# The decays' low-rank map as two float32 products, with the weights W and mu W, in a diffusion trunk with RWKV and neighbourhood attention

## The chip, the cores and the metric

The kernel runs on one core of a Trainium2 chip. The metric is the device time of one execution in microseconds (us); of several executions the median is given. TensorE multiplies matrices into PSUM; VectorE and ScalarE work element by element and may read PSUM; GpSimd works element by element on SBUF. The queues of SP and ScalarE issue the transfers. TensorE's clock has two levels here, 1.2 and 2.4 GHz.

## The reference, cut to what matters

The model has two layers, on 512 latent tokens and 128 context tokens of 1024 features. The first layer's mixer is RWKV-7. Its input h is the normalised x, scaled and shifted by the conditioning. Each of six users of h sees its own mixture of h and the difference delta between the neighbours' mean and h:

```python
def rms_norm(x, g):
    y = x32 * lax.rsqrt(jnp.mean(x32 * x32, axis=-1, keepdims=True) + NORM_EPS)
    return (y * g.astype(jnp.float32)).astype(x.dtype)
...
    h = modulate(rms_norm(xs, norm_g[l, 0]), sh1, sc1)
...
    delta = centred_token_shift(h) - h
    xs = h[None] + delta[None] * mu[:, None, None, :]
    rkv = jnp.einsum('ibtd,ide->ibte', xs[:3], w_rkv)
    r, k, v = rkv[0], rkv[1], rkv[2]
    xw, xa, xg = xs[3], xs[4], xs[5]
    g = jax.nn.sigmoid(xg @ g1) @ g2
    for d in range(2):
        z = w0[d] + jnp.tanh(xw @ w1[d]) @ w2[d]
        decay = jnp.exp(-jnp.exp(-jax.nn.softplus(-z) - 0.5))
        a = jax.nn.sigmoid(a0[d] + (xa @ a1[d]) @ a2[d])
```

The change concerns `xw @ w1[d]`, the first factor of the decays' low-rank map. The two directions' 64 columns each stand side by side, so W is 1024 by 128 there. The scan over the tokens, the output projection, the MLP and the second layer (attention and MLP) follow.

## The kernel before, in words

Activations lie with the features on the 128 partitions: a feature block k (KT = 8 of them) of all T = 640 tokens is one 128x640 piece, and a product of weights with them runs as two halves of HALF = 320 tokens, each into a PSUM bank.

Products with large weights are not done in float32. Weights and activations are each cast to a reduced type (`fp32r` in the rows; ScalarE) and the rest is kept as a second such number (VectorE subtracts). `wblock` (L186) loads 512 KB of raw weights through the pool `wraw` of two buffers on SP's queue and makes `whi` and `wlo`; `split` (L243) makes `xh` and `xl`; `fm_step` (L200) multiplies whi with xh, whi with xl, and wlo with xh, 6 matmuls for each block k. The conditioning's products, of which the weights are used once, are plain float32 (L286).

`start_norm` (L418) loads x in four transfers on SP's queue, then sixteen blocks of conditioning weights (512 KB each, six buffers). ScalarE squares x, VectorE sums the squares (L336), TensorE reduces and spreads them (L355, L374), and VectorE scales x (L433). Meanwhile TensorE computes the conditioning, in eight pieces of two half blocks; after each pair, ScalarE writes two blocks of h into `hp` (L446, with a column of zeros at either end), and VectorE makes their delta in `dl` in three steps (L449, L451, L452).

`phase_proj` (L454) then does, in the order of the program: the decays' map (`Lora1(0, 3)`: weights by `wblock`, and for each k a `mix` on VectorE (L475), its split, and `fm_step`); the map's end (tanh on ScalarE, L518); the preparation of the second factor (`lora2`: two raw weight buffers filled by four transfers, casts, subtractions); eight mixed inputs for the keys (`mixed(1)`); and a loop over eight blocks of keys, each with two stages of the decays' second factor (L546, L548), a key product, and one block of the next low-rank map (`Lora1(1, 4)`). The receptance phase, the gate and the values follow, and then the scan.

Mixed inputs live in the pool `xp` (eight pairs); of the users other than the values, every fourth block takes one of two pairs in `xq` instead. Small tiles of these phases come from the pools `evp` and `ev2`, which open before the first map. The order of the instructions on each engine is not the program's order: a planner with a model of the engines' times sorts them by program order among those that are ready, and this order is fixed when the program is built. Thus L475 and L248 stand between the last steps of dl in the trace.

Of the kernel before, what the change touches and what calls it, by code (L numbers as in the profile page):

```python
# [8 lines left out]
F32 = mybir.dt.float32  # L9
# [3 lines left out]
ALU = mybir.AluOpType  # L13
# [3 lines left out]
P = 128  # L17
D = 1024
KT = 8
# [3 lines left out]
HALF = T // 2  # L23
# [149 lines left out]
class K:  # L173
# [241 lines left out]
    def pool(self, st, name, bufs, **k):  # L415
        return st.enter_context(self.tc.tile_pool(name=name, bufs=bufs, reuse_waits="tile", **k))

    def start_norm(self, st, hp, dl):  # L418

        nc = self.nc  # L420
        p2 = self.pool(st, "n1", 2)
        adp = self.pool(st, "adp", 6)
        ps2 = self.pool(st, "n1p", 4, space=PSUM)
        xt = p2.tile([P, KT, T], F32, name="xt", bufs=1)
        xv = self.A["xT"].rearrange("(k p) t -> p k t", p=P)
        for k2 in range(4):
            nc.sync.dma_start(xt[:, 2 * k2:2 * k2 + 2, :], xv[:, 2 * k2:2 * k2 + 2, :])
        self.ada_prepare(p2)
        nc.vector.memset(hp[:, :, 0:1], 0.0)
        nc.vector.memset(hp[:, :, T + 1:T + 2], 0.0)  # L430
        rb = self.rms_bcast(xt, p2)
        for k in range(KT):
            nc.vector.tensor_tensor(xt[:, k, :], xt[:, k, :], rb, op=ALU.mult)  # L433
        gs = self.const.tile([P, 8, 2], F32, name="gs00")
        m = self.mods[0]
        for j in range(4):
            for b in (4 + j, j):
                ps = ps2.tile([P, 512], F32, name="adp")
                self.ada_second(*self.ada_first(0, b, adp, ps[:, :256]), ps[:, 256:260])
            ks = slice(2 * j, 2 * j + 2)  # L440
            nc.vector.scalar_tensor_tensor(gs[:, ks], m[:, 8 + 2 * j:10 + 2 * j], 1.0,
                                           self.par("norm_g")[:, ks].unsqueeze(2).broadcast_to([P, 2, 2]),
                                           op0=ALU.add, op1=ALU.mult)
            for k in range(2 * j, 2 * j + 2):
                for a, c, i in ((0, TS, 0), (TS, TP, 1)):
                    nc.scalar.activation(hp[:, k, a + 1:a + 1 + c], xt[:, k, a:a + c], AF.Identity, scale=gs[:, k, i:i + 1],  # L446
                                         bias=m[:, k, i:i + 1])
                s = p2.tile([P, T], F32, name="n_s")
                nc.vector.tensor_tensor(s, hp[:, k, 0:T], hp[:, k, 2:T + 2], op=ALU.add)  # L449

                nc.vector.tensor_copy(s[:, TS - 1:TS + 1], hp[:, k, TS - 1:TS + 3:3])  # L451
                nc.vector.scalar_tensor_tensor(dl[:, k], s, 0.5, hp[:, k, 1:T + 1], op0=ALU.mult, op1=ALU.subtract)  # L452

    def phase_proj(self, sc):  # L454
        nc, tc = self.nc, self.tc
        with ExitStack() as st:
# [4 lines left out]
            hpool = self.pool(hst, "hpool", 1, side="right")  # L461
            hp = hpool.tile([P, KT, T + 2], F32, name="hp")
            dl = hpool.tile([P, KT, T], F32, name="dl")
            with ExitStack() as s2:
                self.start_norm(s2, hp, dl)
            pst0.close()
            psx = ExitStack()
            self.psl = self.pool(psx, "psl", 5, space=PSUM)
            self.wraw = pool("wraw", 2)
            xp = pool("xp", 8)  # L470
            mu = self.par("mu")

            def mix(m, k):
                t = mp.tile([P, T], F32, name="mixt")
                nc.vector.scalar_tensor_tensor(t, dl[:, k], mu[:, m * 8 + k:m * 8 + k + 1], hp[:, k, 1:T + 1],  # L475
                                               op0=ALU.mult, op1=ALU.add)
                return self.split(xq if m != 2 and k % 4 == 3 else xp, t)

            mixed = lambda m: [mix(m, k) for k in range(KT)]
            s3 = ExitStack()  # L480
# [4 lines left out]
            self.whl = self.pool(s3, "whl", 3)  # L485
            l2 = self.pool(s3, "l2", 1)
            self.cst2_load(l2)
            evp = self.pool(s3, "evp", 1)
            ev2 = self.pool(s3, "ev2", 2)
            half = l2.tile([P, 48], F32, name="half")  # L490
            for j, n in enumerate(("w0", "a0")):
                nc.vector.tensor_scalar(half[:, 16 * j:16 * j + 16], self.par(n), 0.5, None, op0=ALU.mult)
# [8 lines left out]
            class Lora1:  # L501


                def __init__(s_, j, m):
                    s_.j, s_.m = j, m
                    s_.w = self.wblock(self.A["lora1"][j])
                    s_.ps = self.fm_tiles()

                def step(s_, k):
                    self.fm_step(s_.ps, s_.w, mix(s_.m, k), k, KT)  # L510

                def end(s_):
                    lw = evp.tile([P, T], F32, name="lw")
# [9 lines left out]
            def lora2(lw, j):  # L523

                X, W = [], []
                lo = l2.tile([P, D], F32R, name="l2lo")
                for d in range(2):
                    o, q = slice(64 * d, 64 * d + 64), slice(64 - 64 * d, P - 64 * d)
                    x = l2.tile([P, T], F32R, name=f"l2x{d}")
                    nc.scalar.copy(x[o], lw[o])  # L530
                    nc.vector.tensor_tensor(x[q], lw[o], x[o].bitcast(F32), op=ALU.subtract)
                    raw = self.wraw.tile([P, D], F32, name="wraw")
                    for h in range(2):
                        nc.sync.dma_start(raw[64 * h:64 * h + 64], self.A["lora2"][j, d])
                    w = l2.tile([P, D], F32R, name=f"l2w{d}")
                    nc.scalar.copy(w, raw)
                    nc.vector.tensor_tensor(lo[o], raw[o], w[o].bitcast(F32), op=ALU.subtract)
                    X.append(x)
                    W.append(w)

                def stage(pr, d, out):
                    c = slice(pr * P, (pr + 1) * P)
                    o = slice(64 * d, 64 * d + 64)
                    ps = [pst.tile([P, 512], F32, name=f"st{g}")[:, :HALF] for g in range(2)]
                    for g in range(2):
                        nc.tensor.matmul(ps[g], lhsT=W[d][:, c], rhs=X[d][:, G2[g]], start=True, stop=False)  # L546
                    for g in range(2):
                        nc.tensor.matmul(ps[g], lhsT=lo[o, c], rhs=X[d][o, G2[g]], start=False, stop=True)  # L548
                    b = half[:, 16 * j + 8 * d + pr:16 * j + 8 * d + pr + 1]
                    for g in range(2):  # L550
                        nc.scalar.activation(out(g), ps[g] if j else ps[g].rearrange("p (w t) -> p w t", t=64),
                                             AF.Tanh, bias=b, scale=0.5)
                return stage
# [6 lines left out]
            lora = Lora1(0, 3)  # L560
            for k in range(KT):
                lora.step(k)
            w_stage = lora2(lora.end(), 0)

            xs = mixed(1)
# [1002 lines left out]
```

## Time and profile before

| what | value |
|---|---|
| median of 3 runs | 2248.33 us (2247.55 to 2261.33) |
| profiled execution | 2250.36 us |
| its span, first to last instruction | 2248.5 us |
| mean granted clock of TensorE | 0.945 |
| TensorE matmuls busy | 2007.7 us (89%) |
| VectorE busy | 1180.0 us (52%) |
| ScalarE busy | 866.0 us (39%) |
| GpSimd busy | 463.8 us (21%) |

Busy shares are means over stages of different kinds. PE is TensorE, PEld its weight loads, DVE VectorE, ACT ScalarE, POOL GpSimd, SP the sync engine with its queue. Matmuls overlap in time, so their pace is read from start to start (the pitch), not from one's duration. A float32 matmul appears as two instructions, a reduced one as one. Times in rows are counted from the span's start.

### The profile page before, as it was taken

The numbers are of one execution on the slowest core, as the hardware profiler recorded it, in microseconds if no ns is written. First come the engines' busy times: TensorE is split into PE (matmuls) and PEld (weight loads), VectorE is DVE, ScalarE is ACT, GpSimd is POOL, SyncE is SP. The second block draws the span as 40 slices with busy tenths as digits, with TensorE's granted clock in tenths as the row PEclk, the third lists the DMA queues.
The fourth block names the chain that finished last, engine by engine and source line by source line (L and its number), as shares of the span: only waits on it lengthen the run. The fifth ranks groups of instructions, "written<-read, shape, count | busy, mean of one in ns | idle before, by whom it ended". The sixth has DMA issues, their size and how long they took to land.

```text
span 2248.5 us, 44838 instructions
## 1 busy us (share of the span) xinstructions
PE 2007.7 (89%) x18516; PEld 1823.6 (81%) x18516; DVE 1180.0 (52%) x2587; ACT 866.0 (39%) x1735; POOL 463.8 (21%) x558
## 2 busy tenths in 40 slices
PE   5898978757665677999999999999999999999999
PEld 3787877646554566999999998888777999999999
DVE  6847667396687766433333334434566643434342
ACT  3544554356553425413131323221576331313130
POOL 0001257566552323101010110000232210101010
PEclk9897989888888798999999999999899999999999
DMA  6454864444443455323232223433311232222221
GB/s 232 123 154 140 251 204 158 141 149 148 131 130 121 101 181 164 94 75 113 76 104 75 94 75 114 137 116 108 111 58 29 75 123 75 75 76 74 74 75 70
DMA packets 161388, 260.01 MB, mean 116 GB/s; under 512 B 46880, under 2 KB 103328, under 8 KB 161184
## 3 DMA queue, kind: packets, MB, share of 16 engines
q1 hardware_dynamic: 146816, 240.37, 34.2%
q10 hardware_dynamic: 14368, 16.78, 2.3%
q8 instruction: 145, 2.38, 0.4%
q14 instruction: 59, 0.48, 0.1%
HBM read 218.18 MB, written 37.35 MB: 114 GB/s over the span
## 4 chain that ended last, share of the span: by engine, by line
PE 73%; DVE 13%; DMA 6%; ACT 3%; POOL 2%; issue 2%; SPq 1%; ACTq 0%; DVEq 0%; POOLq 0%
PE psl L205 53%; PE psl L239 4%; PE ps L1495 2%; DVE invT L973 2%; DVE invX L976 2%; PE po L1532 2%; PE pp L832 2%; POOL C L927 2%; PE pt L1520 2%; DVE C L957 1%; PE psl L286 1%; DMA ld_s<-scr 1%; PE pp L1199 1%; DMA wi<-scr 1%; PE st L548 1%
## 5 line engine op out<-in xcount | busy, mean ns | idle before, releaser
L191 ACT CAST whi<-wraw 128x1024 fp32r<-128x1024 f32 x179 | 187.2, 1048 | 730.9 <-PE psl L205 702.5
L205 PE MATMUL psl<-xh,whi 128*128 128x320 f32 (+1 forms) x1712 | 419.8, 318 | 20.8 <-ACT whi L191 15.1
L205 PE MATMUL psl<-xl,whi 128*128 128x320 f32 (+1 forms) x1712 | 417.0, 316 | 7.9 <-DVE xl L248 7.9
L205 PE MATMUL psl<-xh,wlo 128*128 128x320 f32 (+1 forms) x1712 | 415.0, 315 | 2.6 <-DVE wlo L193 2.6
L205 PEld LDWEIGHTS psl<-xh,whi 128*128 128x128 f32 x1712 | 295.4, 192 | 39.4 <-ACT whi L191 19.3
L205 PEld LDWEIGHTS psl<-xl,whi 128*128 128x128 f32 x1712 | 296.3, 192 | 13.9 <-DVE xl L248 10.0
L205 PEld LDWEIGHTS psl<-xh,wlo 128*128 128x128 f32 x1712 | 297.1, 192 | 5.2 <-DVE wlo L193 3.0
L1152 DVE SCALAR_TENSOR_TENSOR xres<-psl,mods,xres 128x320 f32<-128x320 f32 (+2 forms) x216 | 81.7, 434 | 305.5 <-PE psl L205 305.5
L1315 POOL TENSOR_TENSOR relu<-relu 128x640 f32<-128x640 f32 x64 | 80.8, 1263 | 753.1 <-ACT relu L1314 736.2
L205 PE MATMUL psl<-hhh,wlo 128*128 128x320 f32 x1024 | 233.5, 309 | 0.0
L205 PE MATMUL psl<-hhh,whi 128*128 128x320 f32 x1024 | 233.2, 309 | 0.0
L205 PE MATMUL psl<-hhl,whi 128*128 128x320 f32 x1024 | 233.2, 309 | 0.0
L193 DVE TENSOR_TENSOR wlo<-wraw,whi 128x1024 fp32r<-128x1024 f32 x179 | 222.5, 1245 | 14.2 <-ACT whi L191 14.0
L205 PEld LDWEIGHTS psl<-hhh,whi 128*128 128x128 f32 x1024 | 171.2, 188 | 0.4 <-issue 0.4
L205 PEld LDWEIGHTS psl<-hhl,whi 128*128 128x128 f32 x1024 | 171.1, 188 | 0.0
L205 PEld LDWEIGHTS psl<-hhh,wlo 128*128 128x128 f32 x1024 | 171.1, 188 | 0.0
L1272 DVE TENSOR_TENSOR relu<-psl,rms_b 128x320 f32<-128x320 f32 x128 | 60.7, 486 | 144.4 <-PE psl L205 143.3
L832 PE MATMUL pp<-C,KB 128*64 128x128 f32 x1280 | 97.6, 298 | 27.2 <-DVE C L957 13.1
L248 DVE TENSOR_TENSOR hhl<-relu,hhh 128x640 fp32r<-128x640 f32 x64 | 53.4, 834 | 127.9 <-ACT hhh L247 127.8
L832 PEld LDWEIGHTS pp<-C,KB 128*64 128x64 f32 x1280 | 79.9, 149 | 41.3 <-issue 20.7
L957 DVE TENSOR_TENSOR C<-pp,cstsb 64x512 f32<-64x512 f32 x80 | 55.1, 689 | 76.5 <-ACT C L954 68.9
L1032 ACT ACTIVATE GU<-A 32x256 f32<-32x256 f32 x160 | 60.0, 375 | 84.3 <-DVE mods L300 51.8
(288 smaller groups left out, 3389.7 us busy)
## 6 DMA issues: line engine op xcount, KB each, us to landing
wraw<-in_mlp_w SPq DMA_DIRECT2D x128, 512.0 KB, 3.5
adaraw<-in_ada_w SPq DMA_DIRECT2D x96, 512.0 KB, 4.9
ld_d<-scr SPq DMA_DIRECT2D x20, 512.0 KB, 4.1
ld_s<-scr SPq DMA_DIRECT2D x20, 512.0 KB, 3.9
bias<-in_bias SPq DMA_DIRECT2D x16, 384.0 KB, 3.5
scr<-ta SPq DMA_DIRECT2D x16, 325.0 KB, 3.5
wi<-scr SPq DMA_DIRECT2D x20, 260.0 KB, 4.5
scr<-bp SPq DMA_DIRECT2D x16, 320.0 KB, 4.6
```

The costliest lines, as they stand in the source:

```text
L191: nc.scalar.copy(hi, raw)
L193: nc.vector.tensor_tensor(lo, raw, hi.bitcast(F32), op=ALU.subtract)
L205: self.nc.tensor.matmul(ps[g][:, :e - c], lhsT=a[:, k, :], rhs=b[:, c:e], start=(k == 0 and j == 0), stop=(k == n - 1 and j == 2))
L239: nc.tensor.matmul(ps, lhsT=a[:, tc_], rhs=w, start=(k == 0 and j == 0), stop=(k == KT - 1 and j == 2))
L248: (lo_eng or nc.vector).tensor_tensor(xl, src, xh.bitcast(F32), op=ALU.subtract)
L832: r = (op or self.nc.tensor.matmul)(*a, **k)
L927: nc.gpsimd.tensor_tensor(rev(o) if s == 0 else o, v4(sh, s, ww)[hs], f[hs], op=ALU.mult)
L957: nc.vector.tensor_tensor(C[o, 8 * h:8 * h + 8, :], pn[o, :, 0:64], mask[o], op=ALU.mult)
L1032: nc.scalar.activation(gu[64 - 64 * hp:96 - 64 * hp, hp, pp].rearrange("p b v -> p (b v)"), U[32 * q:32 * q + 32, :], AF.Copy, scale=-0.5)
L1152: nc.vector.scalar_tensor_tensor(out[:, a:b], ps[g][:, o:o + b - a], gate[:, k, j:j + 1], x[:, a:b], op0=ALU.mult, op1=ALU.add)
L1272: nc.vector.tensor_tensor(t[:, c], ps[q][:, :HALF], rb[:, c], op=ALU.mult)
L1315: nc.gpsimd.tensor_tensor(t, t, t, op=ALU.mult)
```

## The change

W of the decays' map is loaded raw on SP's queue in `start_norm`, between x and the conditioning's weights, into one of two new tiles (4 KB for each partition) on the side of SBUF where hp and dl lie. GpSimd multiplies it by mu (one factor for each feature, the same for 128 columns) into the other. The map's product is then W with h plus mu W with delta, both in float32, 32 matmuls in all, straight from hp and dl; no mix, no cast and no split of weights or inputs is made for it. The two tiles are given back after the product, and `evp` and `ev2` open behind that.

```diff
-    def start_norm(self, st, hp, dl):
+    def start_norm(self, st, hp, dl, w0):
...
             nc.sync.dma_start(xt[:, 2 * k2:2 * k2 + 2, :], xv[:, 2 * k2:2 * k2 + 2, :])
+        nc.sync.dma_start(w0[0], self.A["lora1"][0])
         self.ada_prepare(p2)
...
+            mu = self.par("mu")
+            w0st = ExitStack()
+            w0p = self.pool(w0st, "w0p", 1, side="right")
+            w0 = [w0p.tile([P, KT, P], F32, name=f"w0{i}") for i in range(2)]
             with ExitStack() as s2:
-                self.start_norm(s2, hp, dl)
+                self.start_norm(s2, hp, dl, w0)
+            nc.gpsimd.tensor_tensor(w0[1], w0[0], mu[:, 24:32].unsqueeze(2).broadcast_to([P, KT, P]), op=ALU.mult)
...
-            evp = self.pool(s3, "evp", 1)
-            ev2 = self.pool(s3, "ev2", 2)
...
                 def __init__(s_, j, m):
                     s_.j, s_.m = j, m
-                    s_.w = self.wblock(self.A["lora1"][j])
+                    s_.w = self.wblock(self.A["lora1"][j]) if j else w0
                     s_.ps = self.fm_tiles()
 
                 def step(s_, k):
-                    self.fm_step(s_.ps, s_.w, mix(s_.m, k), k, KT)
+                    if s_.j:
+                        self.fm_step(s_.ps, s_.w, mix(s_.m, k), k, KT)
+                        return
+                    for j, (w, x, o) in enumerate(((s_.w[0], hp, 1), (s_.w[1], dl, 0))):
+                        for g in range(2):
+                            nc.tensor.matmul(s_.ps[g][:, :HALF], lhsT=w[:, k, :], rhs=x[:, k, o + HALF * g:o + HALF * g + HALF],
+                                             start=(k == 0 and j == 0), stop=(k == KT - 1 and j == 1))
...
             for k in range(KT):
                 lora.step(k)
+            w0st.close()
+            evp = self.pool(s3, "evp", 1)
+            ev2 = self.pool(s3, "ev2", 2)
             w_stage = lora2(lora.end(), 0)
```

## Rows read from the trace of the kernel before

**Rows 1.** By stretch: length; busy (count) of PE, PEld, DVE, ACT, POOL; clock; DMA

```profile
15.21:44.00 28.79, 27.95 (x173) 16.36 (x173) 14.74 (x45) 9.66 (x21) 0.00 (x0) 1.00 0.65 239
44.00:58.48 14.48, 2.96 (x6) 1.44 (x7) 14.48 (x25) 7.19 (x12) 0.00 (x0) 1.00 0.28 73
58.48:74.18 15.70, 11.80 (x45) 10.71 (x46) 14.39 (x17) 7.34 (x10) 0.00 (x0) 0.79 0.58 166
74.18:93.05 18.87, 18.05 (x74) 13.48 (x74) 18.01 (x31) 14.04 (x26) 0.00 (x0) 0.82 0.36 113
93.05:150.00 56.95, 56.95 (x379) 48.84 (x377) 24.42 (x44) 21.79 (x39) 0.00 (x0) 1.00 0.45 139
```

**Rows 2.** Chain that ended last, from 14 to 64 us: start, length, what held it

```profile
14.33 0.84 DVE sqa L336
15.21 2.29 PE psl L355 x10
...
58.96 4.07 DMA wraw<-in_lora
```

**Rows 3.** VectorE in order of time: start, duration, line, operation, xcount

```profile
52.67 1.56 DVE L452 SCALAR_TENSOR_TENSOR dl<-n_s,hp 128x640 f32<-128x640 f32 x2
54.15 1.55 DVE L248 TENSOR_TENSOR xl<-mixt,xh 128x640 fp32r<-128x640 f32 x2
55.62 1.67 DVE L475 SCALAR_TENSOR_TENSOR mixt<-dl,parsb,hp 128x640 f32<-128x640 f32 x2
57.21 1.22 DVE L193 TENSOR_TENSOR wlo<-wraw,whi 128x1024 fp32r<-128x1024 f32 x1
```

**Rows 4.** TensorE in order of time, 63 to 84 us

```profile
63.45 0.73 PE L205 MATMUL psl<-xh,wlo 128*128 128x320 f32 x2
63.98 0.51 PE L205 MATMUL psl<-xh,whi 128*128 128x320 f32 x2
64.33 0.45 PE L205 MATMUL psl<-xl,whi 128*128 128x320 f32 x2
64.62 0.46 PE L205 MATMUL psl<-xh,wlo 128*128 128x320 f32 x2
...
74.18 0.73 PE L205 MATMUL psl<-xh,whi 128*128 128x320 f32 x2
...
80.22 0.73 PE L546 MATMUL st<-l2x,l2w 128*128 128x320 f32 x2
...
82.03 0.42 PE L546 MATMUL st<-l2x,l2w 128*128 128x320 f32 x1
...
83.06 0.41 PE L548 MATMUL st<-l2x,l2lo 64*128 64x320 f32 x1
```

**Rows 5.** Float32 matmuls of 256 columns: start and length; durations min/median/max

```profile
1517.71 1.02 PE L1426 MATMUL psl<-vsh,cst 128*128 128x256 f32 x4
...
L1426 PE MATMUL psl<-vsh,cst x16: 378/379/379, 1517.7 to 1571.6; 128*128 128x256 f32 x16
```

**Rows 6.** Conditioning matmuls: durations min/median/max, first and last start

```profile
L286 PE MATMUL psl<-adaraw,condp x384: 379/379/637, 891.0 to 1848.3; 128*32 128x256 f32 x192
...
L286 PE MATMUL adp<-adaraw,condp x128: 604/634/637, 13.6 to 41.4; 128*32 128x256 f32 x128
```

**Rows 7.** ScalarE in order of time, at the map's end

```profile
75.50 0.76 ACT L518 ACTIVATE lw<-psl 128x320 f32<-128x320 f32 x2
```

**Rows 8.** Busy time around the first weight blocks; a wait of TensorE

```profile
13.40:15.30 1.90, 1.18 (x9) 0.33 (x9) 1.65 (x2) 0.66 (x1) 0.00 (x0) 1.00 1.03 412
...
PE adp L286 <- DMA adaraw<-in_ada_w: 13.6, 1, 13.6
```

**Rows 9.** A GpSimd product's durations; VectorE and GpSimd in time near 914 us

```profile
L621 POOL TENSOR_TENSOR ke<-ta,ta x8: 1564/1587/2163, 211.3 to 290.3; 128x640 f32<-128x640 f32 x8
...
914.23 1.09 DVE L248 TENSOR_TENSOR hhl<-relu,hhh 128x640 fp32r<-128x640 f32 x1 [2.78 <-ACT hhh L247]
...
912.18 2.47 POOL L1315 TENSOR_TENSOR relu<-relu 128x640 f32<-128x640 f32 x2 [29.12 <-ACT relu L1314]
```

More of the change, by code (lines that the diff above doesn't have):

```diff
@@ L470, in phase_proj @@
             xp = pool("xp", 8)
-            mu = self.par("mu")
             def mix(m, k):
```

## The prediction

> **What bounds the kernel now.** I read first the busy time by stretch, then the chain of work that ended last, then each engine's instructions in order of time from 40 to 95 us. In the stretches [rows 1] the reader is to see three regimes. Until 44 us TensorE is nearly always busy, with the conditioning product. From 44.00 to 58.48 VectorE is busy for all 14.48 us and TensorE for 2.96; from 58.48 to 93.05 VectorE is still busy for 32.4 of 34.6 us, and TensorE works partly at half clock. From 93.05 on TensorE is busy for all of the stretch, and VectorE for 24.42 of 56.95 us. In the chain [rows 2] the reader is to see two places that the change touches: the sums of squares that release TensorE at 15.21, and a wait of 4.07 us for low-rank weights within VectorE's stretch. So work taken off VectorE before 93 us is worth time, as far as TensorE can keep up; work added to TensorE is paid where it is late.
>
> By 93.05 TensorE has done three things: the decays' product (48 matmuls, in 24 pairs), the first block of the key projection (24 pairs, the first at 74.18) and six stages of the second low-rank factor (24 matmuls, L546 and L548); the stretch from 74.18 to 93.05 counts 74, two at its edges among them [rows 1, 4]. From there its order is dense, so I ask when the changed kernel stands at the same point.
>
> **What is removed.** VectorE loses 8 mixes (L475), 8 low parts (L248) and one low weight (L193). Two low parts take 1.47 us from start to start, two mixes 1.59, the low weight 1.22 [rows 3]: 4 x (1.47 + 1.59) + 1.22 = 13.5 us. ScalarE loses 8 casts and one weight cast; it is busy 7.2, 7.3 and 14.0 us in the three stretches [rows 1], so I cost that at nothing; VectorE's busy time covers it, and without that cover it would be a further gain. TensorE loses the 48 split matmuls. A transfer of 512 KB moves from the third stretch to the head of SP's queue, and with it one user of the two raw weight buffers: the four half-block loads of the second factor and the next map's weights no longer queue behind it. The chain's 4.07 us in a low-rank weight load [rows 2] may shrink; I count nothing for it, since VectorE was busy in it.
>
> **What is added on TensorE.** 32 float32 products of 320 columns. The trace shows a float32 product as two instructions. With 128 rows and 256 columns at full clock four instructions take 1.02 us and one lasts 0.379, so they start (1.02 - 0.38)/3 = 0.21 us apart; the whole 1.02 divided by four is 0.26 [rows 5]. At 320 columns that is 0.27, at most 0.32; I take 0.27 to 0.30. At half clock it is double, as a pair of split matmuls goes from 0.29 to 0.53 us [rows 4]: 0.53. So all 64 instructions cost 17 to 19 us at 2.4 GHz and 34 us at 1.2 GHz, against 7.1 us for 48 split matmuls at full clock and 12.7 at half.
>
> Which level holds? The granted clock row gives 1.00 before 67 us, but the durations say otherwise: a conditioning matmul takes 634 ns here and 379 later [rows 6], and a pair of split matmuls goes from 0.53 us pitch to 0.29 at 63.98, after 5.5 us of unbroken matmuls from 58.48 [rows 4]. So I take half clock when the product begins and, by that one row of full-size matmuls without a break, full clock 5.5 us later.
>
> The product needs dl. Its last block is done at 54.2 us now [rows 3], behind two mixes that go, so at about 52.6; those before it come some 1.6 us apart. From 44.0 to 49.5 TensorE does 5.5/0.53 = 10 instructions, then 54 at 0.27 to 0.30, 14.6 to 16.2: the end is at 64 to 65.7, and dl is never late after the start. The rest up to the same point is 24 pairs at 0.29 and 24 stage matmuls at 0.34 (82.03 to 83.06 for three steps [rows 4]), 7.0 + 8.2 = 15.2 us. By TensorE the point comes at 79.3 to 80.9. Between the product's end and the first stage lie tanh, two casts and two subtractions, from 75.50 to 80.22 now [rows 4, 7], 4.7 us; the key block's 7.0 us on TensorE cover it. If the key block's mixed inputs were late, it would cost up to 4.7.
>
> **By VectorE** the point comes at 93.05 - 13.5 = 79.6 us. The two bounds agree within a microsecond; VectorE is no longer clearly first, and what is late next is TensorE. I take the upper TensorE value, 80.6.
>
> **The other parts.** The new load stands on SP's queue between the four input loads and the sixteen weight blocks of the conditioning. The transfers run at 412 GB/s there [rows 8], so 512 KB (0.524 MB) take 1.3 us, and each of the sixteen loads behind it can be late by that. The first conditioning matmul at 13.6 waits for its block [rows 8], and the sums of squares come to TensorE at 15.21; 1.0 us of work (eight instructions) slides behind them. Later TensorE is behind the loads. The lowest cost is 0, the highest 1.3; I take 1.0. GpSimd's product (128 by 1024, two inputs) has no row of its own; from 128x640 rows of 1.24 (2.47 for two) and 1.59 us [rows 9] I estimate 2.0 to 2.5 us. It starts when the weights land, near 13.6 us, and is wanted at 44, so 28 us cover it; uncovered it would cost its 2.5. Nothing is queued behind it on GpSimd before 211 us [rows 9]. evp and ev2 open later: their first writer but two 0.07 us memsets is the end of the same product, so nothing.
>
> GpSimd beside VectorE is a term of its own. In one row a low part took 1.09 us instead of 0.82 while two GpSimd products ended beside it [rows 9], so a delay of 0.27 is seen; the nearest case here are the last two sums of squares, of 0.84 us each, that release TensorE at 15.21 [rows 2]. I take 0 (the slot is mostly hidden behind the late block) and keep up to 1.8, should the sum at 14.33 wait until 16.1. The Trainium skill (SBUF — State Buffer, section "SBUF: two separate sides") says that a GpSimd instruction and a VectorE instruction with two SBUF inputs exclude each other for a whole instruction; by that the forecast would be some 0.8 us later, since the delay lies partly beside that of the load. The low part's row agrees in direction.
>
> **Sum.** 80.6 + 1.0 = 81.6 instead of 93.05: 11.4 us earlier. The later phases wait for what this one leaves, and TensorE is busy for all of 93.05 to 150 [rows 1], so the shift is kept. The profiled execution took 2250.4 us around a span of 2248.5, so 2239.0; it stands 2.0 us above the median of 2248.3, for which I forecast **2237 us**.
>
> **Rivals.** *The gain is partly given back* (17%). The order is planned over the whole program, and other placements, VectorE gaps before dl, a missed cover of the 4.7 us or 1.8 us at the head take 4 to 11 us back. For it: two engines are both near their limit at 80 us. Against: ScalarE and the transfers have room [rows 1]. 2242 to 2248.
>
> *The clock stays low* (13%): slower. If TensorE stays at 1.2 GHz through the float32 product, it ends at 45 + 34.1 = 79.1, and with 15.2 behind it the point is 94.3, 1.3 us later than now; if the key block is also half cold, another 3 to 7. It decides once some 56 of the 64 instructions run at 0.53 us, since each beyond my ten costs 0.25 and 11.4 us are there to lose. For it: 29 us of busy TensorE before 44 stayed at half clock [rows 1, 6], and after the gap at 65 us the matmuls went back to it until 80 [rows 1, 4]. Against: those conditioning matmuls use 32 columns of the array, and the only run of full-size ones sped up in 5.5 us. 2250 to 2256.
>
> *A larger gain* (8%). The clock rises early, the product ends at 62, VectorE's bound falls with the waits for low-rank weights (4.07 us [rows 2]) and the load costs nothing: 13 to 20 us, 2228 to 2235.
>
> That the compiled program is the old one in effect is no case: the operations differ.
>
> **Numbers.** The forecast has 62%, with its own range of 2232 to 2242. With the other cases the range is 2228 to 2253. One per cent is 22.5 us, about what a measurement here can tell from no change. Only gains of twice the sum, or a replanned order, cross it: faster 0.07, within 0.88, slower 0.05.
>
> **What would show it.** In the changed profile: 64 float32 instructions of 320 columns from about 44 to 65 us, with pitches of 0.53 falling to 0.27-0.30 after some 5 us; the first dense stretch of the key projection at about 81 instead of 93; VectorE without the 17 instructions and with dl complete near 53; GpSimd's product ended by 17 us; the first conditioning matmul near 15. The prediction is wrong if the pitch stays at 0.53, if dl is late, if the conditioning ends more than 2 us later, or if the lead at 93 us is gone by 300.

## The result, and the profile after

| | median | lowest to highest | runs |
|---|---|---|---|
| before | 2251.57 us | 2245.38 to 2261.33 | 12 |
| after | 2241.03 us | 2232.05 to 2250.45 | 12 |

The ratio is 0.9948 with a 95% interval of 0.9927 to 0.9968: some 0.5% faster, less than the one per cent of which the prediction gives the chances, but clear of no change. The medians stand 10.5 us apart; the forecast was a shift of 11.4, to 2237 us. Of the 4.0 us between 2237 and 2241.0, 3.2 are the median of before, which was 2248.33 us in three runs and is 2251.57 in twelve. The profiled execution of after took 2243.0 us, with a span of 2241.2.

These are the stretches of after at the borders of [rows 1], in the same columns: length; busy (count) of PE, PEld, DVE, ACT, POOL; granted clock; DMA share and GB/s.

```profile
15.21:44.00 28.79, 23.89 (x180) 13.82 (x180) 17.25 (x48) 10.29 (x22) 0.82 (x1) 0.88 0.72 257
44.00:58.48 14.48, 14.48 (x49) 10.07 (x49) 14.48 (x24) 7.09 (x10) 0.00 (x0) 0.88 0.32 78
58.48:74.18 15.70, 13.50 (x72) 11.07 (x71) 15.10 (x22) 9.54 (x14) 0.00 (x0) 1.00 0.48 146
74.18:93.05 18.87, 18.87 (x114) 15.12 (x113) 11.96 (x23) 9.97 (x17) 0.00 (x0) 1.00 0.57 163
93.05:150.00 56.95, 56.95 (x363) 47.23 (x362) 21.70 (x42) 23.54 (x42) 0.00 (x0) 1.00 0.48 142
```

The reader is to see three things. VectorE's full stretch ends earlier: from 74.18 to 93.05 it is busy for 11.96 us instead of 18.01. TensorE is busy where it stood idle, 14.48 us instead of 2.96 in the second stretch. And the clock is 1.00 from 58.48 to 150 us, where [rows 1] has 0.79 and 0.82 up to 93.05 (in a second profile of after it is 0.89 from 58.48 to 74.18). The 0.79 counts the time up to the clock's first record, at 64.1 us, as full, where the durations show half.

TensorE of after in order of time (start, duration, line, operation, count, and in brackets the idle time before it with what ended that). L519 is the float32 product, L205 the key block, L556 the first stage of the second factor.

```profile
16.76 2.30 PE L355 MATMUL psl<-cstsb,sqa 128*128 128x2 f32 x10 [16.76 <-DVE sqa L336]
...
43.26 1.02 PE L296 MATMUL adp<-cstsb,adasb 128*128 128x2 f32 x4 [1.79 <-ACT adasb L289]
44.14 2.48 PE L519 MATMUL psl<-hp,w 128*128 128x320 f32 x4
46.41 1.74 PE L519 MATMUL psl<-dl,w 128*128 128x320 f32 x4
47.98 1.24 PE L519 MATMUL psl<-hp,w 128*128 128x320 f32 x4
49.06 1.24 PE L519 MATMUL psl<-dl,w 128*128 128x320 f32 x4
...
62.00 1.24 PE L519 MATMUL psl<-dl,w 128*128 128x320 f32 x4
63.08 0.59 PE L685 MATMUL pk<-cstsb,cst 128*128 128x256 f32 x2
65.47 0.56 PE L205 MATMUL psl<-xh,whi 128*128 128x320 f32 x2 [1.79 <-ACT whi L191]
...
71.96 0.46 PE L556 MATMUL st<-l2x,l2w 128*128 128x320 f32 x2
```

The product stands between 44.14 and 63.08, 18.9 us for 64 instructions. Four of them take 2.27 us at first (46.41 - 44.14), then 1.57, then 1.08, which is 0.27 each. The key block, where the projection's dense stretch begins, follows at 65.47.

How far after is ahead is best read where a phase is finished. The keys are copied out of PSUM in 16 instructions; before comes first, then after (durations min/median/max, first and last start):

```profile
L580 DVE COPY ke<-psl x16: 481/492/493, 93.1 to 165.2; 128x320 f32<-128x320 f32 x16
```
```profile
L593 DVE COPY ke<-psl x16: 481/492/492, 77.3 to 153.2; 128x320 f32<-128x320 f32 x16
```

The first copy is 15.8 us earlier, but that is partly another order (key matmuls now stand ahead of stages); the last copy, after the same work, is 12.0 us earlier. The same five marks of every kernel follow, each from one profile, in us from the span's start: the start of the sums' reduction (L355 in after), the last of the small matmuls that end the conditioning (L296), the last copy of keys, the first GpSimd sum behind the key phase (L621 in [rows 9]), and the last copy of values. The twelve times of one kernel lie 16 to 18 us apart, so differences between marks, counted from the conditioning's end, tell more of this phase than one time does.

| kernel | ratio to before [95%] | reduction | conditioning ends | last key copy | first sum | last value copy |
|---|---|---|---|---|---|---|
| before | | 15.2 | 43.3 | 165.2 | 211.3 | 410.9 |
| before_again | 1.0005 [0.9987, 1.0023] | 15.2 | 39.9 | 162.1 | 207.9 | 408.1 |
| after | 0.9948 [0.9927, 0.9968] | 16.8 | 43.9 | 153.2 | 196.8 | 400.3 |
| after_again | 0.9966 [0.9951, 0.9981] | 16.8 | 43.4 | 154.2 | 197.7 | 400.1 |
| e1_old_vector_work | 1.0036 [1.0008, 1.0065] | 16.7 | 42.9 | 173.9 | 217.4 | 419.7 |
| e2_early_load_only | 0.9980 [0.9955, 1.0005] | 15.2 | 42.4 | 161.0 | 205.8 | 405.6 |
| e3_scale_on_scalar | 0.9942 [0.9911, 0.9973] | 15.3 | 40.1 | 149.3 | 192.8 | 398.0 |
| e4_second_map_float32 | 0.9946 [0.9929, 0.9963] | 16.7 | 44.1 | 163.4 | 196.3 | 397.7 |
| e5_product_twice | 1.0003 [0.9984, 1.0021] | 16.9 | 44.2 | 168.3 | 212.0 | 415.6 |
| e7_two_maps_scalar | 0.9925 [0.9899, 0.9951] | 15.3 | 40.4 | 158.9 | 191.4 | 391.6 |
| e8_three_maps_scalar | 0.9913 [0.9890, 0.9937] | 15.2 | 41.3 | 159.4 | 194.9 | 388.0 |
| e9_shared_mix | 0.9994 [0.9961, 1.0028] | 15.2 | 40.1 | 155.5 | 196.0 | 395.0 |
| e10_filler | 1.0046 [1.0012, 1.0080] | 15.2 | 40.3 | 165.3 | 210.3 | 417.7 |
| e11_third_raw_buffer | 0.9993 [0.9969, 1.0018] | 15.1 | 40.2 | 161.7 | 201.2 | 403.3 |

Below, "key phase" is the last key copy minus the conditioning's end, and "to the first sum" is that mark minus the same end. Over the two profiles each, before has 122.1 and 168.0 us (means of 121.9 and 122.2, 168.0 and 168.0), after 110.1 and 153.6 (of 109.3 and 110.8, 152.9 and 154.3): 12.0 and 14.4 us are gained.

### The profile page after: what moved, and what is told of

The parts are those of the page before. It is cut to its first block, busy times and chain, and to the rows that moved or that the text cites. A ratio compares the mean times of both kernels' runs of the same rounds, so it can differ in the third digit from the quotient of the medians.

```text
span 2241.2 us, 44842 instructions
## 1 busy us (share of the span) xinstructions
PE 2012.2 (90%) x18532; PEld 1826.7 (82%) x18532; DVE 1172.2 (52%) x2568; ACT 860.1 (38%) x1728; POOL 467.9 (21%) x559
## 4 chain that ended last, share of the span: by engine, by line
PE 73%; DVE 14%; DMA 5%; issue 3%; POOL 2%; ACT 2%; SPq 0%; ACTq 0%; DVEq 0%; POOLq 0%
PE psl L205 53%; PE psl L239 4%; DVE invX L989 3%; PE ps L1508 2%; DVE invT L986 2%; PE pp L845 2%; PE po L1545 2%; PE pt L1533 2%; POOL C L940 1%; PE pp L1212 1%; DVE C L970 1%; PE psl L286 1%; DMA wi<-scr 1%; PE st L558 1%; PE pk L691 1%
## 5 line engine op out<-in xcount | busy, mean ns | idle before, releaser
L205 PE MATMUL psl<-xh,whi 128*128 128x320 f32 (+1 forms) x1696 | 412.9, 316 | 16.4 <-ACT whi L191 10.0
L205 PE MATMUL psl<-xl,whi 128*128 128x320 f32 (+1 forms) x1696 | 408.5, 313 | 1.2 <-DVE xl L248 1.2
L205 PE MATMUL psl<-xh,wlo 128*128 128x320 f32 (+1 forms) x1696 | 407.7, 313 | 0.4 <-DVE ta L585 0.4
L205 PEld LDWEIGHTS psl<-xh,whi 128*128 128x128 f32 x1696 | 289.6, 190 | 35.8 <-ACT whi L191 13.9
L205 PEld LDWEIGHTS psl<-xl,whi 128*128 128x128 f32 x1696 | 291.0, 190 | 5.6 <-issue 3.2
L205 PEld LDWEIGHTS psl<-xh,wlo 128*128 128x128 f32 x1696 | 291.2, 190 | 3.2 <-issue 1.7
L1328 POOL TENSOR_TENSOR relu<-relu 128x640 f32<-128x640 f32 x64 | 80.6, 1261 | 754.3 <-ACT relu L1327 749.6
L205 PE MATMUL psl<-hhh,wlo 128*128 128x320 f32 x1024 | 233.4, 309 | 0.0
L205 PE MATMUL psl<-hhh,whi 128*128 128x320 f32 x1024 | 233.3, 309 | 0.0
L205 PE MATMUL psl<-hhl,whi 128*128 128x320 f32 x1024 | 233.2, 309 | 0.0
L205 PEld LDWEIGHTS psl<-hhh,whi 128*128 128x128 f32 x1024 | 171.1, 188 | 0.4 <-issue 0.4
L205 PEld LDWEIGHTS psl<-hhl,whi 128*128 128x128 f32 x1024 | 171.2, 188 | 0.0
L205 PEld LDWEIGHTS psl<-hhh,wlo 128*128 128x128 f32 x1024 | 171.1, 188 | 0.0
L845 PE MATMUL pp<-C,KB 128*64 128x128 f32 x1280 | 102.8, 312 | 40.0 <-DVE C L970 17.7
L845 PEld LDWEIGHTS pp<-C,KB 128*64 128x64 f32 x1280 | 85.8, 158 | 52.9 <-issue 25.9
```

The source lines that it names most:

```text
L205: self.nc.tensor.matmul(ps[g][:, :e - c], lhsT=a[:, k, :], rhs=b[:, c:e], start=(k == 0 and j == 0), stop=(k == n - 1 and j == 2))
L845: r = (op or self.nc.tensor.matmul)(*a, **k)
L1328: nc.gpsimd.tensor_tensor(t, t, t, op=ALU.mult)
```

## The experiments

The theory is that of the prediction: the gain is VectorE's 13.5 us, and TensorE is the bound behind it. There are two rivals: the gain comes from the clock, because 64 instructions in a row bring TensorE to 2.4 GHz and keep it there; or it comes from the load, which left the queue of the two raw weight buffers.

**The old work on VectorE again.** The eight mixes, their casts and their low parts are made again and not used.

```diff
                 def step(s_, k):
+                    mix(s_.m, k)
                     if s_.j:
```

> The float32 product stays; the eight mixes, casts and low parts of before are made again beside it and used by nobody (only the low weight of 1.2 us stays away). Theory V (the gain is VectorE's freed time in the stretch where it bounds): 8 x 1.53 = 12.2 us come back on VectorE, so the key projections run no earlier than before and the time is that of before within 4 us, the last key copy starting at 163 to 167 us (165.2 before, 153.2 after). Theory B (the gain is the raw weight buffers and transfers freed from the third stretch): the gain stays, the last key copy at 153 to 156, about 2241 us. Theory C (the gain is TensorE's clock, which the dense product raises at 47 us and which was at half until 80 us before): most of it stays too, the last key copy at 154 to 158.

The ratio rose to 1.0036 [1.0008, 1.0065], and this interval does not meet that of after: with the work put back on VectorE (and the eight casts on ScalarE) the whole gain is gone. But the key phase became 131.0 us, 20.9 longer than in after, for 4 x (1.47 + 1.59) = 12.2 us of work on VectorE, and the last key copy came at 173.9, later than any theory had it. Two stretches and one row of TensorE of this kernel show the rest (columns as above).

```profile
58.48:74.18 15.70, 9.96 (x29) 6.04 (x28) 14.45 (x22) 10.21 (x16) 0.00 (x0) 0.79 0.48 143
74.18:93.05 18.87, 18.87 (x49) 12.98 (x49) 11.62 (x22) 9.28 (x17) 0.00 (x0) 0.50 0.37 106
```
```profile
68.31 0.90 PE L557 MATMUL st<-l2x,l2w 128*128 128x320 f32 x2 [5.38 <-DVE l2x L542]
```

TensorE waits 5.38 us for a split input that VectorE delivers late, and then goes at 0.50 although it is busy without a break: 49 matmuls from 74.18 to 93.05 where after has 114. The delay is paid as a wait, and the matmuls behind the wait take longer at the lower clock; why the clock stayed there is not shown. So neither theory is alone in this number.

**Only the load moved.** The load and the pools stand as in after; the product is the old one.

```diff
-    def wblock(self, src):
-        raw = self.wraw.tile([P, KT, P], F32, name="wraw")
-        self.nc.sync.dma_start(raw, src)
+    def wblock(self, src, raw=None):
+        if raw is None:
+            raw = self.wraw.tile([P, KT, P], F32, name="wraw")
+            self.nc.sync.dma_start(raw, src)
...
-                    s_.w = self.wblock(self.A["lora1"][j]) if j else w0
+                    s_.w = self.wblock(self.A["lora1"][j], None if j else w0[0])
```

> The weights of the map are loaded early and the pools stand as after, but the product is the old one: mixed and split inputs, and weights cast and split from the early tile. Theory V: VectorE has all its old work, no gain but for a wait or two: last key copy at 162 to 167 us, time that of before within 4 us. Theory B: the gain is here, last key copy at 153 to 157, 2240 to 2243 us. Theory C: no gain, as TensorE waits as before.

0.9980 [0.9955, 1.0005]: not told apart from no change, and not clear of after's interval either. That the early load is not the gain by itself is shown by the kernel with the old work, which has this load and is no faster than before. The key phase is 118.6 us here, 3.5 shorter than before's, and 163.4 to the first sum, 4.6 shorter. I had counted nothing for it.

The load has a price at the head. The reduction still starts at 15.2, but the eight conditioning matmuls that stood ahead of it now stand behind it. TensorE in before, then in this kernel (its L297 is L296 of before):

```profile
13.62 1.08 PE L286 MATMUL adp<-adaraw,condp 128*32 128x256 f32 x8 [13.62 <-DMA adaraw<-in_ada_w]
...
20.15 1.02 PE L296 MATMUL adp<-cstsb,adasb 128*128 128x2 f32 x4
```
```profile
17.37 3.64 PE L287 MATMUL adp<-adaraw,condp 128*32 128x256 f32 x32
20.94 1.01 PE L297 MATMUL adp<-cstsb,adasb 128*128 128x2 f32 x4
```

The first small matmuls are 0.8 us later, where I had put 1.0. At the conditioning's end this no longer shows: it is 42.4 here, 40.1 and 40.3 in two further kernels with the same early load (e9_shared_mix, e10_filler), and 43.3 and 39.9 in before. That end moves with the clock: of the 128 conditioning matmuls, none ran at the upper level in the first profile of before and 64 in the second, by their durations.

**The scaling on ScalarE.** mu W is made by eight activations instead of one GpSimd product.

```diff
-            nc.gpsimd.tensor_tensor(w0[1], w0[0], mu[:, 24:32].unsqueeze(2).broadcast_to([P, KT, P]), op=ALU.mult)
+            for k in range(KT):
+                nc.scalar.activation(w0[1][:, k, :], w0[0][:, k, :], AF.Copy, scale=mu[:, 24 + k:25 + k])
```

> mu W is made by ScalarE in eight instructions instead of GpSimd in one. If the 1.5 us by which the last sums of squares were late after (4.18 us for three instead of 2.68, first reduction on TensorE at 16.76 instead of 15.21) come from GpSimd holding VectorE up, they go: three sums in 2.7 us, first reduction at 15.2 to 15.4. If they come from the load that stands in front, they stay: 16.7. The time is 0 to 2 us under that of after in the first case, too little to be told from the times alone; the last key copy at 151.5 to 153.

The sums of squares in order of time, in after and then in this kernel (start and total duration of three, with the GpSimd product beside them in after):

```profile
12.53 4.18 DVE L336 TENSOR_TENSOR sqa<-sqa,sq 128x640 f32<-128x640 f32 x3
...
13.66 2.36 POOL L471 TENSOR_TENSOR w<-w,parsb 128x1024 f32<-128x1024 f32 x1 [13.22 <-DMA w<-in_lora]
```
```profile
12.53 2.68 DVE L336 TENSOR_TENSOR sqa<-sqa,sq 128x640 f32<-128x640 f32 x3
```

The three sums take 1.50 us more while GpSimd multiplies. The longest of the six in after is the row's maximum, 2329 ns against a median of 824:

```profile
L336 DVE TENSOR_TENSOR sqa<-sqa,sq x6: 819/824/2329, 9.3 to 14.4; 128x640 f32<-128x640 f32 x6
```
```profile
L336 DVE TENSOR_TENSOR sqa<-sqa,sq x6: 819/826/827, 9.3 to 14.4; 128x640 f32<-128x640 f32 x6
```

The reduction follows at 16.8 instead of 15.3. The table bears it out for every kernel: the five profiles with a GpSimd product (after twice, e1, e4, e5) have the reduction at 16.7 to 16.9 and the conditioning's end at 42.9 to 44.2, mean 43.7; the nine without have 15.1 to 15.3 and 39.9 to 43.3, mean 40.9. The first small matmuls, at which the clock has not yet risen or only just, part the two costs: they start at 20.06 to 20.15 us in the three profiles without the early load, at 20.80 to 20.94 in the six with the load and no GpSimd product, and at 22.50 to 22.65 in the five with both. That is 0.8 us for the load and 1.7 for the product. By time, 0.9942 and after's 0.9948 aren't told apart.

**The product made twice.** The 64 instructions run a second time into the same sums.

```diff
-                    for j, (w, x, o) in enumerate(((s_.w[0], hp, 1), (s_.w[1], dl, 0))):
+                    for j, (w, x, o) in enumerate(((s_.w[0], hp, 1), (s_.w[1], dl, 0)) * 2):
...
-                                             start=(k == 0 and j == 0), stop=(k == KT - 1 and j == 1))
+                                             start=(k == 0 and j == 0), stop=(k == KT - 1 and j == 3))
```

> The float32 product is made twice into the same banks (the map's output is doubled, the rest is as after), 64 more instructions, 17.3 us of TensorE at 0.27. If TensorE bounds the stretch from 44 us on after the change, as the prediction has it, nearly all of it shows: last key copy at 167 to 171 us (153.2 after), time 2254 to 2260, some 14 to 17 us over after. If VectorE still bounds there (it was busy for 14.48 and 15.10 us of the stretches 44.00 to 58.48 and 58.48 to 74.18 after), TensorE's waits of 1.8 and 0.4 us and the mixes that can go ahead take up part: 8 to 12 us over after.

Of 64 x 0.27 = 17.3 us added on TensorE the key phase shows 14.0 (124.1 against 110.1), the first sum 14.2, and the ratio 0.0055 x 2251.6 = 12.4 us (0.0037, 8.3 us, against after_again). So TensorE does bound the phase after the change, by most of what is added; some 3 us of slack were left, among them the 1.79 and 0.41 us that it stands idle in after at 63.7 to 66.7 and that this kernel does not have.

**The second map too.** The map behind the decays' also takes two float32 products.

```diff
+    def wmu(self, m):
+        raw = self.whl.tile([P, KT, P], F32, name="whi")
+        self.nc.sync.dma_start(raw, self.A["lora1"][1])
+        w = self.whl.tile([P, KT, P], F32, name="wlo")
+        self.nc.gpsimd.tensor_tensor(w, raw, self.par("mu")[:, 8 * m:8 * m + 8].unsqueeze(2).broadcast_to([P, KT, P]), op=ALU.mult)
+        return raw, w
...
-                    if s_.j:
+                    if s_.j == 2:
```

> The next map (a's first factor, in the key phase) is treated the same way: two float32 products, no mixes and splits. Theory V with TensorE as the bound from 80 us on: 64 float32 instructions at 0.27 are 17.3 us against 48 at 0.147, 7.1 us, so the key phase is 8 to 10 us longer than after, less what waits at its end: last key copy at 159 to 164, time 2243 to 2251. If VectorE still bounded there, or the fixed gain of leaving mixes out carried over, it would be faster than after by 5 to 12 us: 2229 to 2236.

The key phase grew by 9.2 us (119.3), about as priced: 17.3 for the product less 7.1 for the split one. But the time did not: 0.9946, as after. The copies of keys and then the first GpSimd sums of this kernel and of after show where it came back.

```profile
L600 DVE COPY ke<-psl x16: 473/482/492, 77.0 to 163.4; 128x320 f32<-128x320 f32 x16
...
L641 POOL TENSOR_TENSOR ke<-ta,ta x8: 1565/1581/2144, 196.3 to 276.9; 128x640 f32<-128x640 f32 x8
```
```profile
L634 POOL TENSOR_TENSOR ke<-ta,ta x8: 1558/1583/2160, 196.8 to 278.6; 128x640 f32<-128x640 f32 x8
```

The keys are 10.2 us later than in after and the first sum is 0.5 earlier. From 93.05 to 150 us VectorE is busy for 14.35 us here and for 21.70 in after, so it comes to the next phase with less still to do; that this is what shortens the hand-over is argued, not shown by a run of its own. I had followed the cost to the end of its own phase and no further; the expectation of a slower kernel was wrong.

**Both findings together.** Two maps in float32 with the scaling on ScalarE, then all three. The diff is from the kernel above to the three maps; that of two keeps the split product for the third.

```diff
-        self.nc.gpsimd.tensor_tensor(w, raw, self.par("mu")[:, 8 * m:8 * m + 8].unsqueeze(2).broadcast_to([P, KT, P]), op=ALU.mult)
+        for k in range(KT):
+            self.nc.scalar.activation(w[:, k, :], raw[:, k, :], AF.Copy, scale=self.par("mu")[:, 8 * m + k:8 * m + k + 1])
...
-                    s_.w = w0 if j == 0 else self.wmu(m) if j == 1 else self.wblock(self.A["lora1"][j])
+                    s_.w = self.wmu(j, m) if j else w0
...
-                    if s_.j == 2:
-                        self.fm_step(s_.ps, s_.w, mix(s_.m, k), k, KT)
-                        return
```

> The first two maps in float32, both mu W by ScalarE. The run with the second map on GpSimd lost 10.2 us by the last key copy (163.4 against 153.2) and had them back by the first sum in the receptance phase (196.3 against 196.8), so VectorE's mixes that go are worth time where the key phase hands over. With ScalarE in place of GpSimd neither the sums of squares (1.5 us) nor the mixes at 44 to 47 us are held up: last key copy at 158 to 162, first GpSimd sum at 190 to 195, time 2232 to 2239. If the hand-over is bound by the second factor's weight load instead, it gives nothing over ScalarE in the first map alone: 2237 to 2241.

> All three low-rank maps in float32. The third runs in the receptance phase, where VectorE is busy for 20.9 of 30 us from 200 to 230 us and 16.3 from 230 to 260, TensorE for 28.5 and 29.5 (before). If TensorE bounds that phase, 17.3 - 7.1 = 10.2 us come on top of two maps, and VectorE's 12.2 us give back at most the hand-over to the gate: 3 to 10 us slower than two maps. If VectorE's mixes bound the receptance phase, it is 3 to 8 us faster than two maps.

0.9925 [0.9899, 0.9951] and 0.9913 [0.9890, 0.9937]: the three-map kernel has the lowest median of all that ran, 2232.66 us. Its interval overlaps that of the two maps and a little that of after, and is clear of after_again's. By the last copy of values, counted from the conditioning's end, they stand at 351.2 and 346.7 us, where before has 367.9 and after 356.6 (means of two). The third product runs behind the key phase, from 161 to 188 us; the key phases themselves are alike (118.1 and 118.5). Of the two expectations for it, the one by which it costs 3 to 10 us on TensorE did not come: by the last copy of values the three maps are 4.5 us ahead, though not by a clear difference in time. TensorE is kept busy behind the keys. From 150 to 200 us, after and then the three maps (columns as above):

```profile
150.00:200.00 50.00, 44.02 (x190) 35.09 (x189) 37.25 (x55) 25.06 (x42) 3.12 (x2) 0.73 0.44 127
```
```profile
150.00:200.00 50.00, 49.55 (x262) 39.19 (x261) 35.05 (x52) 28.40 (x54) 3.13 (x2) 1.00 0.47 139
```

The 50 us hold 262 matmuls instead of 190, at a clock of 1.00 instead of 0.73. VectorE's work and TensorE's clock improve together, as in the change itself, and this run does not part them either.

**Before and after once more,** to see how far the marks of one kernel move.

> The changed kernel once more, for how far its marks vary from one profiled execution to another. All theories: the three last sums of squares take 4.2 us again and TensorE's first reduction comes at 16.6 to 16.9, since the order is fixed; the last key copy within 2 us of 153.2, varying with the moment at which the clock rises in the conditioning; time within 0.3 per cent of 2241.

> The kernel before once more, for how far its marks vary: last key copy within 2 us of 165.2, first reduction of the sums of squares at 15.2, and the clock's fall to half near 67 us and rise near 80, moved by a few us at most. Ratio 1 within 0.3 per cent.

Before again is 1.0005, and after again 0.9966 [0.9951, 0.9981]: the gain repeats, and its two intervals overlap. The key phase agrees to 0.3 us in the two profiles of before and to 1.5 in those of after, while before's conditioning ends 3.4 us apart.

**No mixes, but the split product.** From the early-load kernel: the decays' map is fed by the mixed inputs of the keys. So VectorE loses the eight mixes and low parts, and TensorE keeps 48 split matmuls.

```diff
-                    self.fm_step(s_.ps, s_.w, mix(s_.m, k), k, KT)
+                    self.fm_step(s_.ps, s_.w, mix(s_.m, k) if s_.j else xs[k], k, KT)
...
+            xs = mixed(1)
             lora = Lora1(0, 3)
```

> As the run with the early load alone, but the first map's split product takes the keys' mixed inputs (its own mixes, casts and low parts are left out, so the map sees another mixture). It takes 12.2 us from VectorE without the float32 product. The run with the early load alone had its last key copy at 161.0 us. Theory V: 161.0 less 9 to 12, at 149 to 152, below the 153.2 of the changed kernel, as TensorE has 7.1 us of split matmuls in place of 17.3. Theory C (the dense float32 product keeps the clock up, and that is the gain): little, 158 to 161.

Against the early-load kernel the key phase is 3.2 us shorter (115.4 and 118.6) and the way to the first sum 7.5 (155.9 and 163.4). The last key copy, at 155.5, lies between the two expectations, and the time, 0.9994 [0.9961, 1.0028], shows no gain. Taking work off VectorE alone therefore gives less than its length. The float32 product needs some 12 us more of TensorE (18.9 against 7.1) and still ends the phase 5.3 us sooner. TensorE of this kernel at the points where it differs:

```profile
50.84 0.90 PE L206 MATMUL psl<-xl,whi 128*128 128x320 f32 x2 [5.40 <-DVE xl L249]
...
59.47 0.56 PE L206 MATMUL psl<-xl,whi 128*128 128x320 f32 x2 [1.59 <-DVE xl L249]
...
62.46 0.90 PE L206 MATMUL psl<-xh,whi 128*128 128x320 f32 x2 [1.85 <-ACT whi L192]
...
67.43 0.73 PE L206 MATMUL psl<-xh,whi 128*128 128x320 f32 x2
```

It waits 5.40 us for the first low part, where after has its product under way from 44.14, and then in smaller pieces for split inputs and weights. From 63.16 to 68 a pair has a pitch of 0.53: half clock.

**The clock without the change.** From the early-load kernel: three matmuls that nobody reads stand behind each of the eight steps.

```diff
+                        for _ in range(3):
+                            nc.tensor.matmul(s_.idle[:, :HALF], lhsT=w0[0][:, k, :], rhs=hp[:, k, 1:1 + HALF], start=True, stop=True)
```

> As the run with the early load alone, with three float32 matmuls of 320 columns (1.6 us at full clock) put behind each of the eight steps of the first map, into a bank that nobody reads: TensorE is as dense as with the change, VectorE does all its old work. Theory C: TensorE stays at full clock from about 55 to 80 us and the last key copy comes 3 to 8 us before 161.0. Theory V: the clock may stay up, but the key block waits for VectorE as before, and the last key copy is at 160 to 163.

The clock did rise where the fillers are, and fell again behind them:

```profile
58.48:74.18 15.70, 13.82 (x69) 11.11 (x70) 15.24 (x19) 8.57 (x13) 0.00 (x0) 1.00 0.33 100
74.18:93.05 18.87, 16.97 (x58) 12.73 (x57) 14.57 (x26) 10.67 (x19) 0.00 (x0) 0.64 0.34 106
```

The key phase is 125.0 us, longer than the 118.6 without fillers, and the ratio 1.0046 [1.0012, 1.0080]; neither theory had expected a longer one. The fillers have a price of their own, 48 instructions or some 14 us of TensorE, and behind them the clock is 0.64 where before has 0.82. So this run does not decide on the clock theory. The early-load kernel says more. It has VectorE's old work, and this stretch:

```profile
74.18:93.05 18.87, 18.22 (x94) 14.05 (x93) 17.92 (x33) 13.03 (x23) 0.00 (x0) 1.00 0.48 147
```

With the clock full there, its key phase is 3.5 us shorter than before's, not 12.0: with VectorE's work left in, the clock in that stretch is not the gain. What the clock is worth once VectorE is free, no run says.

**The load theory by itself.** Before, with a third raw weight buffer.

```diff
-            self.wraw = pool("wraw", 2)
+            self.wraw = pool("wraw", 3)
```

> The kernel before with three raw weight buffers instead of two from the first map to the values, and nothing else. Counted from the end of the conditioning (its last small matmul on TensorE), the last key copy came 121.9 and 122.2 us later in two profiles of the kernel before and 118.6 later with the early load. Theory B in part (the early load's 3.4 us are the raw buffer that the first map no longer holds): 118 to 119.5 here too. If they are the clock's place on the key block alone, as it was at full in 74 to 93 us in that run: 121 to 123, with TensorE at half clock somewhere between 65 and 85 us, or below 120 only with full clock there.

0.9993 [0.9969, 1.0018], and a key phase of 121.5 us, 0.6 from before's. So the third buffer is not what shortens the early-load kernel's key phase by 3.5; the way to the first sum is 7.0 us shorter (161.0 against 168.0), which the time does not show. What made those 3.5 us stays open. The granted clock from 74.18 to 93.05 is a candidate, not a proof: 0.82 and 0.88 in the two profiles of before, 0.93 here and 1.00 with the early load, beside key phases of 121.9, 122.2, 121.5 and 118.6.

## Why the prediction was right, point by point

**The stretch that VectorE bounds gets shorter, and TensorE is late next.** Right. The points of the sum were a gain of 12.4 us behind the conditioning, less 1.0 at the head (the 80.6 in it is called TensorE's upper value, which is 80.9 where it is worked out). The key phase gained 12.0. That VectorE's work counts is shown by putting it back, which turned 0.9948 into 1.0036; that TensorE is the bound after it, by the doubled product, of whose 17.3 us 14.0 appear. That the size fits so well is partly luck: 3.5 of the 12.0 us came with the early load alone, for which no gain was counted. Not shown is that VectorE's work is all of it: without the mixes but with the split product 3.2 to 7.5 us came, with fillers nothing. What fits all the runs is that both halves of the edit count: less work on VectorE, and a product that needs no split input from it, so that TensorE works from 44 us on with 2.2 us of waits and is mostly at its upper level. That reading is argued from these runs; none of them gives the clock's share by itself.

**The size of the product.** Nearly. It took 18.9 us where 20 to 21.7 were forecast, from 44.0 to between 64 and 65.7 (17 to 19 was for the full clock alone). At full clock the pitch is 0.27, the lower end of what I took from [rows 5]. The slow part was shorter: about 3 us instead of 5.5, so the product ended at 63.2 us (62.00 + 1.24). The row I took it from [rows 4] had one case of such a rise. The granted clock row can be trusted here: it gives 0.50 from 44 to 47 us and 0.93 from 47 to 50.

**The shift input in time.** Right. dl is complete at 51.41 + 1.56 = 52.97 (forecast: near 53) and TensorE never waits for it.

**The cover of 4.7 us.** Nearly. The key block does stand between the product and the first stage, and no wait for the map's end shows on TensorE. But its own weights came late, and TensorE stood for 1.79 and 0.41 us. ScalarE's cast of the first key block waited for the transfer:

```profile
64.37 1.04 ACT L191 CAST whi<-wraw 128x1024 fp32r<-128x1024 f32 x1 [1.69 <-DMA wraw<-in_w_k]
```

The time that the short slow part had gained went there. The projection's dense stretch, forecast for about 81 us, began at 66.7, since key matmuls now stand ahead of the stages; so that sign does not measure the lead.

**The head.** The step that failed, with a small price. I gave 1.0 us to the load and 0 to GpSimd beside VectorE, with a bound of 1.8. At the first small matmuls the load costs 0.8 us, and GpSimd's product 1.7 instead of 0; the sums of squares take 1.50 us more. The Trainium skill (SBUF — State Buffer, section "SBUF: two separate sides") has the rule that fits: a VectorE instruction with two inputs in SBUF and a GpSimd instruction that reads SBUF exclude each other for a whole instruction. The row of 2329 ns agrees, since GpSimd's 2.36 us begin at 13.66 and end at 16.02, and the sum that started at 14.4 ends at 16.7; the low part of [rows 9], only 0.27 us longer, was no measure of this. The prediction named the rule and took the row. The first conditioning matmul came at 18.99 us, not near 15. What the product costs at the conditioning's end is between nothing (43.3 in one profile of before) and 2.8 us (the difference of the two means above), because that end moves by 3.4 us in before alone. That after's 43.9 lies so near before's 43.3 is luck: 40 of its 128 conditioning matmuls ran at the upper clock, and none in that profile of before.

**Kept to the end.** Within the noise. In the two single profiles the lead is 12.0 us at the last key copy, 14.5 at the first sum, 10.6 at the last value copy and 7.3 in the spans, while the medians of twelve runs give 10.5. The stages behind 400 us move by 6 us between two profiles of after (spans of 2241.2 and 2247.0), so no loss there is shown.

**Rivals.** The rival in which the clock stays low did not come, though the experiment with the old work has its picture: 0.50 from 74 to 93 us in a busy TensorE, and a kernel slower than before. The place was the stages behind a VectorE delay, not the product. The gain was not given back beyond the noise, though 2241.0 us lies close to that rival's 2242. The larger gain did not come either; three maps reached its range, at 2232.7 us.

## What to carry to other kernels

Where VectorE prepares the operands of a product that TensorE does in little time, a dearer product on operands that already exist can be the cheaper one: here 18.9 us on TensorE replaced some 7.1 there and 13.5 on VectorE, and the phase became 12.0 us shorter, 3.5 of them open. Price each engine's path to the same mark, and follow a cost over the next hand-over before calling it a loss, since the second map's 9.2 us were given back by the phase behind. And look what runs beside a small product that nobody waits for: on GpSimd it held up a sum of squares to 2.33 us, on ScalarE it left them at 0.83.

## What the runs showed of the hardware

The clock in the conditioning was not what [rows 6] led me to think. The same small matmuls rise in the middle of it: in after, eight take 0.64 us at 31.01 and 1.03 at 37.04.

```profile
31.01 0.64 PE L286 MATMUL adp<-adaraw,condp 128*32 128x256 f32 x8
...
37.04 1.03 PE L286 MATMUL adp<-adaraw,condp 128*32 128x256 f32 x8
```

The second profile of before has such a stretch too, from 20.7 to 31.0 us by the granted clock, and the first profile has none; that goes with an end at 39.9 instead of 43.3. The reverse was as unexpected: in the kernel with the old work, TensorE was busy for all of 74.18 to 93.05 us and the granted clock stayed at 0.50. One rise in a trace is a poor guide to the next.
